# The first two feature tiles computed k by k between the adaLN products, with the input scaling on VectorE and the gate weights summed later

## The chip, the cores and the metric

The kernel runs on one core of a Trainium2 chip. The metric is the device time of one execution in microseconds (us); before the change the median of three runs is 2062.04. The engines are TensorE (PE; PEld is its weight load), VectorE (DVE), ScalarE (ACT), GpSimd (POOL), and SyncE (SP), which issues all DMAs here.

## The reference

One block of a diffusion model over 1024 latent tokens and 256 context tokens of width 1024, in two layers. This case lies in the start of the first (mLSTM) layer:

```python
shift, scale, gate = ada(c, w_ada[i], b_ada[i])            # silu(c) @ w + b, split in three
h_lat = modulate(rmsnorm(x, pre_g), shift, scale)          # h * (1 + scale) + shift
h_ctx = modulate(rmsnorm(ctx, pre_g), c_shift, c_scale)
...
xm, z, og = split(h @ w_in, 3)                             # each 2048 wide
xc = silu(short_conv(xm, conv_w, conv_b))
q, k, v = headwise(xc, w_q), headwise(xc, w_k) * DH**-0.5, headwise(xm, w_v)   # 4x4 blocks
pre = concat(q, k, v) @ w_g + b_g                          # gates of the mLSTM
```

Behind that come the mLSTM scans in two directions, the output projection, and a pooling mixer as second layer. All is fp32; a product is done as three matmuls of split operands (high part by high, high by low, low by high).

## The kernel before

**Layout.** Tokens lie along the free dimension: `x_sb[k]` is the k-th of eight tiles of 128 features by 1024 tokens, `c_sb` holds the context. A *feature tile* n (0 to 15) is 128 of the 2048 columns of `xm`; `features(n, side)` (from L349) computes it in three chunks (512, 512 and 256 tokens), each a sum over the eight k in one PSUM bank, three matmuls per k (`mm3`). It then copies the sums out, convolves them (L372 to L375), splits results into high and low parts and stores them.

**Start.** SP loads x, ctx and sixteen adaLN weight tiles, then the weights of feature tiles 0 and 1 (`first_w`). TensorE's order is written by hand for this stage; `PE_START` (L35) lists it:

```python
PE_START = "0 1 t0 L t1 2 SL t2 C 3 4 t3 5 t4 SC 6 t5 7 t6 t7"
```

A digit n is `ada_product(n)`: two rows of shift and scale for feature block n. `tn` is `ada_turn`: the rows, copied to SBUF by ScalarE, are transposed into columns `mod0[:, n]` and `gs0[:, n]`. `L`, `C` are the token sums of squares, `SL`, `SC` spread the reciprocal norms over the partitions. After that list, x is scaled by its norm: tiles 0 to 4 by VectorE from PSUM (L280), tiles 5 to 7 and the context by GpSimd (L276, L282). Then GpSimd sums the gate weights (L295 to L302): three loads of 512 KB, each multiplied by the 4x4 blocks and added up, giving `gx_all` and `gm_all`. `modulate` (L304) makes each k of the layer's input: ScalarE computes the high part from `src * sc + sh` (L307), VectorE the same in fp32 (L308, a TENSOR_SCALAR) and the low part (L312); the fp32 value is stored to `h_d`.

**Tiles.** Tile 0 is summed with k outside and two chunks inside, so that it can follow `modulate`; from tile 1 on one chunk after the other. While tile n runs, `side` inserts the value products of earlier tiles, one step after each k of tile 2 and after every second k of other tiles. This is `token_part` (L388): its right-hand side `vv` is 128 columns of value weights and 16 gate columns copied from `gm_all` (L397). `gacc` are three PSUM banks (tag `pc`) for the other gate sums. `block_sums` (L503) later reads `h_d` back and forms sums of the blocks of the input for a Strassen product.

TensorE's order is fixed by the program text; on the other engines and on SP a scheduler sets one order per engine when the program is built. An engine executes its instructions in that order, waiting on semaphores. Buffers of a tag rotate: `T5` has five (the adaLN weights 0 to 4, later the gate weights and the convolution's inputs and outputs), `wr`, `wh`, `wl` (loaded weights, their high and low parts) two each. PSUM has eight banks: `pa` 3, `pb` 2, `pc` 3.

Of the kernel before, what the change touches and what calls it, by code (L numbers as in the profile page):

```python
# [17 lines left out]
P = 128  # L18
# [34 lines left out]
def hybrid_block(ctx: ExitStack, tc: tile.TileContext, xT, ctxT, vecs, w_ada0, w_ada, w_blk, w_krow, blk_mask, w_gate, w_in, b_gate, w_out,  # L53
# [32 lines left out]
    def pt_(tag, shape=(P, 512)):  # L86
        return ps.tile(list(shape), F32, tag=tag, bufs=PBUFS[tag], name=nm(tag))

    def const(shape, name, dt=F32):
        return sb.tile(list(shape), dt, name=name)  # L90
# [98 lines left out]
        return row  # L189

    def ada_turn(n, row):
        q = pt_("pc", [P, 2, 2])
        for part in range(2):
            PE.transpose(q[:, part], row[:, part], ident[:2, :2])
        for part in range(2):
            S.activation(mod0[:, n, part], q[:, part], AF.Identity, bias=vc("b_ada0", 8 * part + n))
        S.activation(gs0[:, n], mod0[:, n, 1], AF.Identity, scale=vc("a_pre", n), bias=vc("a_pre", n))
# [88 lines left out]
    gsum = tl("T5", [P, 3, KE, 16])  # L286

    def add4(dst, src):
        G.tensor_tensor(dst, src[:, :, 0], src[:, :, 1], op=ALU.add)
        for o in (2, 3):  # L290
            G.tensor_tensor(dst, dst, src[:, :, o], op=ALU.add)

    for i in range(3):
        g4 = tl("T5", [P, KE, 4, 16])
        nc.sync.dma_start(g4, w_gate[i])  # L295
        G.tensor_tensor(g4, g4, wb[:, i, :, :, None].to_broadcast([P, KE, 4, 16]), op=ALU.mult)
        add4(gsum[:, i], g4)
# [17 lines left out]
    h = {}
    for k in range(KD):
        if k < 4:
            if k % 2 == 0:
                quad = [[tl("S4", [P, 2, 512], F32R) for _ in range(2)] for _ in range(2)]
            for hf in range(2):  # L320
                h[k, hf] = tuple(t[:, k % 2] for t in quad[hf])
            modulate(x_sb[k], [(*h[k, hf], slice(512 * hf, 512 * hf + 512)) for hf in range(2)], k, 0, h_d[k])
        else:
            pair = [tl("S4", [P, T], F32R) for _ in range(2)]
            for hf in range(2):
                h[k, hf] = tuple(t[:, 512 * hf:512 * hf + 512] for t in pair)
            modulate(x_sb[k], [(*pair, slice(0, T))], k, 0, h_d[k])
    hch = [tl("S4", [P, 4, TC], F32R) for _ in range(2)]
    hcl = [tl("S4", [P, 4, TC], F32R) for _ in range(2)]
    for k in range(KD):  # L330
        modulate(c_sb[k // 4][:, k % 4], [(hch[k // 4][:, k % 4], hcl[k // 4][:, k % 4], slice(0, TC))], k, 1)
# [8 lines left out]
    def hx(k, ci, lo):  # L340
        if ci < 2:
            return h[k, ci][lo]
        return (hcl if lo else hch)[k // 4][:, k % 4]


    gacc = [pt_("pc") for _ in range(3)]

    def features(n, side):
        wh, wl = first_w[n] if n < 2 else load_w(w_in[n])  # L349
# [6 lines left out]
        if n == 0:  # L356
            ps_ = [pt_("pa") for _ in range(3)]
            for k, ci in [(k, ci) for k in range(KD) for ci in range(2)] + [(k, 2) for k in range(KD)]:
                mm3(ps_[ci][:, :CHUNKS[ci][1]], wh[:, k], wl[:, k], hx(k, ci, 0), hx(k, ci, 1), k == 0, k == KD - 1)
# [142 lines left out]

    def block_sums():  # L503

        for k in range(4):
# [6 lines left out]
            V.tensor_tensor(b11, b22, b11, op=ALU.add)  # L512
            V.tensor_tensor(b21, b21, b11, op=ALU.subtract)
# [758 lines left out]
```

## Time and profile before

| | |
|---|---|
| median of 3 runs (lowest to highest) | 2062.04 us (2061.18 to 2064.16) |
| the profiled execution | 2061.71 us |
| its span | 2059.9 us |
| busy: PE, PEld | 1993.8, 1680.1 us |
| busy: DVE, ACT, POOL | 1244.8, 760.5, 325.9 us |
| mean granted clock of TensorE | 0.986 of full speed |

Times in the profile count from the start of the span. A row of the timeline gives start, duration, engine, source line (L137 is the matmul helper, so matmuls are told apart by their tiles), operation, output and inputs, how many are merged, and in brackets the idle time before with what ended it. Instructions of one engine may overlap a little, so that rows of merged matmuls add up to slightly more than the time that passed.

### The profile page before, as it was taken

Reading aid. Unit: us, or ns where it says so; the run is one execution under the profiler, and the core shown is the slowest. Engines: PE = TensorE matmul, PEld = TensorE weight load, DVE = VectorE, ACT = ScalarE, POOL = GpSimd, SP = SyncE. Lnnn points to the kernel's source line nnn. Section 1 sums busy time; section 2 is a strip of 40 time slices with the busy share of each in tenths; the row PEclk is TensorE's granted clock in tenths of the full one; section 3 lists DMA queues with packets and bytes.
Section 4 is the critical chain, followed back from the end, with each engine's and each line's share of the span. In section 5 each row is a group of like instructions: output and inputs, shape, how many; then the busy total and the mean of one; then the engine's idle time right before and its main releaser. Section 6 shows DMA issues by size and latency. Waiting matters only on the chain.

```text
span 2059.9 us, 26957 instructions
## 1 busy us (share of the span) xinstructions
PE 1993.8 (97%) x10210; PEld 1680.1 (82%) x10210; DVE 1244.8 (60%) x2115; ACT 760.5 (37%) x1225; POOL 325.9 (16%) x399
## 2 busy tenths in 40 slices
PE   7899999999999899999999999999999999999997
PEld 5678788888888688888888878887888888888897
DVE  4866566677777577667676662444747293844444
ACT  5444454433333432333323322433423131223443
POOL 4400000042232000000000001343000000001265
PEclk9999999999999999999999999999999999999999
DMA  8476776864444854648355334534331312133573
GB/s 322 159 255 222 261 241 214 303 196 138 148 129 133 269 181 141 227 132 273 98 166 207 108 97 144 197 114 163 103 104 50 102 51 92 46 126 130 181 242 124
DMA packets 201986, 339.48 MB, mean 165 GB/s; under 512 B 12508, under 2 KB 116444, under 8 KB 201856
## 3 DMA queue, kind: packets, MB, share of 16 engines
q1 hardware_dynamic: 201856, 337.76, 48.8%
q8 instruction: 80, 1.31, 0.3%
q14 instruction: 50, 0.41, 0.1%
HBM read 234.77 MB, written 102.94 MB: 164 GB/s over the span
## 4 chain that ended last, share of the span: by engine, by line
PE 87%; DVE 3%; DMA 3%; POOL 1%; ACT 1%; issue 1%; SPq 0%; DVEq 0%; ACTq 0%; POOLq 0%
PE pa L137 45%; PE pc L137 33%; PE pb L137 7%; PE pb L781 1%; DMA wr<-in_w_ada_dram 1%; POOL hn L969 1%; PE pc L812 1%; DVE S L901 1%; DVE wl L145 1%; DMA wr<-in_w_in_dram 1%; DMA T<-in_bw_out_dram 0%; DMA S<-xl_d 0%; POOL S L989 0%; DVE wl L658 0%; DMA S<-h_d 0%
## 5 line engine op out<-in xcount | busy, mean ns | idle before, releaser
L137 PE MATMUL pa<-S,wh 128*128 128x512 f32 (+1 forms) x2496 | 725.9, 375 | 13.8 <-DVE S L312 7.1
L137 PEld LDWEIGHTS pa<-S,wh 128*128 128x128 f32 x2496 | 447.4, 191 | 88.6 <-DVE S L312 10.8
L137 PE MATMUL pa<-S,wl 128*128 128x512 f32 (+1 forms) x1248 | 462.5, 371 | 3.3 <-DVE wl L145 3.3
L137 PE MATMUL pc<-S,wh 128*128 128x512 f32 (+1 forms) x1616 | 451.4, 365 | 4.4 <-ACT wh L143 3.5
L137 PEld LDWEIGHTS pc<-S,wh 128*128 128x128 f32 x1616 | 292.7, 189 | 54.3 <-ACT wh L143 3.7
L145 DVE TENSOR_TENSOR wl<-wr,wh 128x1024 fp32r<-128x1024 f32 (+1 forms) x124 | 147.5, 1189 | 273.0 <-ACT wh L143 272.1
L137 PE MATMUL pc<-S,wl 128*128 128x512 f32 (+1 forms) x808 | 293.8, 365 | 1.0 <-DVE wl L145 1.0
L137 PEld LDWEIGHTS pa<-S,wl 128*128 128x128 f32 x1248 | 237.6, 190 | 44.0 <-DVE wl L145 3.7
L137 PE MATMUL pa<-S,S 128*128 128x512 f32 (+1 forms) x1152 | 250.9, 363 | 10.1 <-DMA S<-xh_d 5.8
L143 ACT ACTIVATE wh<-wr 128x1024 fp32r<-128x1024 f32 (+1 forms) x124 | 124.6, 1005 | 368.6 <-PE pa L137 148.3
L137 PE MATMUL pc<-S,pt 128*128 128x512 f32 x960 | 227.4, 391 | 1.5 <-DVE S L721 1.1
L137 PEld LDWEIGHTS pa<-S,S 128*128 128x128 f32 x1152 | 191.8, 190 | 40.2 <-DMA S<-xh_d 6.2
L137 PEld LDWEIGHTS pc<-S,pt 128*128 128x128 f32 x960 | 178.2, 188 | 38.5 <-DVE S L721 1.7
L137 PEld LDWEIGHTS pc<-S,wl 128*128 128x128 f32 x808 | 152.9, 189 | 25.7 <-DVE wl L145 1.8
L783 ACT ACTIVATE pt<-pb 128x512 fp32r<-128x512 f32 (+1 forms) x96 | 47.7, 523 | 213.8 <-PE pb L781 208.0
L969 POOL TENSOR_TENSOR hn<-hn,pt 128x512 f32<-128x512 f32 (+1 forms) x48 | 77.5, 1617 | 309.0 <-ACT pt L968 307.9
L740 DVE SCALAR_TENSOR_TENSOR T<-pa,T 128x256 f32<-128x256 f32 (+3 forms) x184 | 78.2, 454 | 33.5 <-PE pa L137 29.3
L137 PE MATMUL pb<-S,wh 128*128 128x512 f32 x256 | 78.8, 389 | 0.0
L570 ACT ACTIVATE wh<-T 128x512 fp32r<-128x512 f32 x70 | 41.2, 627 | 96.4 <-PE pc L137 78.3
L794 DVE BATCH_NORM_STATS2 st<-pc 128x6 f32<-128x512 f32 x32 | 22.4, 699 | 86.4 <-PE pc L137 86.4
L145 DVE TENSOR_TENSOR wl<-T,wh 128x1024 fp32r<-128x1024 f32 x32 | 45.5, 1421 | 47.3 <-ACT wh L143 47.2
L137 PEld LDWEIGHTS pb<-vv,S 128*128 128x128 f32 x384 | 61.6, 190 | 11.8 <-ACT S L369 1.9
(319 smaller groups left out, 2371.5 us busy)
## 6 DMA issues: line engine op xcount, KB each, us to landing
wr<-in_bw_in_dram SPq DMA_DIRECT2D x40, 512.0 KB, 3.5
wr<-in_w_in_dram SPq DMA_DIRECT2D x34, 512.0 KB, 4.9
wr<-in_w_ada_dram SPq DMA_DIRECT2D x32, 512.0 KB, 4.0
wr<-in_w_out_dram SPq DMA_DIRECT2D x32, 512.0 KB, 3.5
T<-in_bw_out_dram SPq DMA_DIRECT2D x32, 512.0 KB, 4.3
S<-y_d SPq DMA_DIRECT2D x28, 512.0 KB, 7.0
vh_d<-T SPq DMA_DIRECT2D x16, 640.0 KB, 4.0
vl_d<-T SPq DMA_DIRECT2D x16, 640.0 KB, 6.3
```

Of the source, the lines that this page charges most:

```text
L137: PE.matmul(out, lhsT, rhs, start=start, stop=stop)
L143: S.activation(h, r, AF.Copy)
L145: V.tensor_tensor(l, r, f(h), op=ALU.subtract)
L570: S.activation(hi, a, AF.Copy)
L740: V.scalar_tensor_tensor(W[:, lo + sh:hi + sh], p[:, lo - o:hi - o], 1.0, W[:, lo + sh:hi + sh], op0=ALU.mult, op1=ALU.mult, accum_out=dp[ ...
L781: PE.transpose(p[:, j], st["M"][:, s * P:(s + 1) * P], ident)
L783: S.activation(th[:, :n], p[:, :n], AF.Copy)
L794: V.bn_stats(b6, pv)
L812: PE.transpose(p[:, c], hn[:, c * P:(c + 1) * P], ident)
L901: V.tensor_tensor(b, yraw[kp, hf], f(a), op=ALU.subtract)
L969: G.tensor_tensor(acc, acc, sq, op=ALU.add)
```

## The change

- `PE_START` gets steps `F0` to `F7`, one for each k, between and behind the last adaLN products, and each turn comes directly behind its product. `F`k is `early(k)`: it modulates k (latent and context) and adds its part to tiles 0 *and* 1, so six PSUM banks (`pa` and `pc`) are in use at once; `ada_turn` moves from `pc` to `pb`.
- The scaling passes L276, L280 and L282 go. `modulate` multiplies by scale and norm in one SCALAR_TENSOR_TENSOR on VectorE; ScalarE adds the shift for the high part; a second SCALAR_TENSOR_TENSOR gives the low part. `h_d` now holds the value without its shift, which `block_sums` adds.
- The gate weights become a function, called after tile 1; `gacc` is allocated there too.

```diff
-KP = 5
-PE_START = "0 1 t0 L t1 2 SL t2 C 3 4 t3 5 t4 SC 6 t5 7 t6 t7"
+PE_START = "0 1 t0 L t1 2 SL t2 C 3 t3 SC 4 t4 F0 5 t5 F1 6 t6 F2 7 t7 F3 F4 F5 F6 F7"
...
     def ada_turn(n, row):
-        q = pt_("pc", [P, 2, 2])
+        q = pt_("pb", [P, 2, 2])
...
+    def modulate(src, r, parts, k, j, dst=None):
+        sc, sh = gs0[:, k, j:j + 1], mod0[:, k, 0, j:j + 1]
+        V.scalar_tensor_tensor(src, src, sc, r, op0=ALU.mult, op1=ALU.mult)
+        if dst is not None:
+            nc.sync.dma_start(dst, src)
+        for hi, _, c in parts:
+            S.activation(hi, src[:, c], AF.Identity, bias=sh)
+        for hi, lo, c in parts:
+            V.scalar_tensor_tensor(lo, src[:, c], sh, f(hi), op0=ALU.add, op1=ALU.subtract)
...
+    def early(k):
...
+        modulate(x_sb[k], rs_xs, parts, k, 0, h_d[k])
+        modulate(c_sb[k // 4][:, k % 4], rs_cs, [(hch[k // 4][:, k % 4], hcl[k // 4][:, k % 4], slice(0, TC))], k, 1)
+        for n in range(2):
+            if k == 0:
+                ps_[n] = [pt_("pc" if n else "pa") for _ in range(3)]
+            for ci in range(3):
+                mm3(ps_[n][ci][:, :CHUNKS[ci][1]], first_w[n][0][:, k], first_w[n][1][:, k], hx(k, ci, 0), hx(k, ci, 1),
+                    k == 0, k == KD - 1)
...
+        elif step[0] == "F":
+            early(int(step[1]))
...
-    for k in range(KP, KD):
-        G.tensor_tensor(x_sb[k], x_sb[k], rs_xs, op=ALU.mult)
-    for k in range(KP):
-        for ci in range(2):
-            o = ci * 512
-            V.tensor_tensor(x_sb[k][:, o:o + 512], x_sb[k][:, o:o + 512], rs_ps[ci], op=ALU.mult)
-    for k in range(2):
-        G.tensor_tensor(c_sb[k], c_sb[k], rs_cs[:, None, :].to_broadcast([P, 4, TC]), op=ALU.mult)
+
+    def gate_weights():
+        gsum = tl("T5", [P, 3, KE, 16])
...
-    def modulate(src, parts, k, j, dst=None):
-        sc, sh = gs0[:, k, j:j + 1], mod0[:, k, 0, j:j + 1]
-        for hi, _, c in parts:
-            S.activation(hi, src[:, c], AF.Identity, bias=sh, scale=sc)
-        V.tensor_scalar(src, src, sc, sh, op0=ALU.mult, op1=ALU.add)
...
-        for hi, lo, c in parts:
-            V.tensor_tensor(lo, src[:, c], f(hi), op=ALU.subtract)
...
-            V.tensor_tensor(b22, b22, b12, op=ALU.subtract)
+            V.scalar_tensor_tensor(b22, b22, dsh[:, k], b12, op0=ALU.add, op1=ALU.subtract)
...
             out = features(n, side)
             for _ in side:
                 pass
+            if n == 1:
+                gacc.extend(pt_("pc") for _ in range(3))
+                gate_weights()
```

The order of the instructions changes at three places that the prediction uses.

SP, behind the start's loads, before. `S_1_100`, `S_2_102`, ... are the x tiles that go to `h_d`, `T_78_460`, `T_79_466`, `T_80_472` the gate weights, `wr_788` and `wr_1043` the weights of tiles 2 and 3:

```order
L247 DMA bg<-in_b_gate_dram 128x16
L295 DMA T_78_460<-in_w_gate_dram 128x1024
L310 DMA h_d<-S_1_100 128x1024
L310 DMA h_d<-S_2_102 128x1024
L310 DMA h_d<-S_4_106 128x1024
L141 DMA wr_788<-in_w_in_dram 128x1024
L295 DMA T_79_466<-in_w_gate_dram 128x1024
L295 DMA T_80_472<-in_w_gate_dram 128x1024
L141 DMA wr_1043<-in_w_in_dram 128x1024
```

and with the change, where `wr_1214` and `wr_1402` are the weights of tiles 4 and 5, `T_123_749`, `T_124_755`, `T_125_761` the gate weights, `T_107_695` and `T_115_728` the convolved tiles 0 and 1:

```order
L266 DMA h_d<-S_11_120 128x1024
L140 DMA wr_1214<-in_w_in_dram 128x1024
L140 DMA wr_1402<-in_w_in_dram 128x1024
L330 DMA T_123_749<-in_w_gate_dram 128x1024
L377 DMA xc_d<-T_107_695 128x1024
L385 DMA xh_d<-S_109_702 128x1024
L386 DMA xh_d<-pt_701 128x256
L330 DMA T_124_755<-in_w_gate_dram 128x1024
L385 DMA xl_d<-S_110_703 128x1024
L386 DMA xl_d<-pt_701 128x256
L377 DMA xc_d<-T_115_728 128x1024
L330 DMA T_125_761<-in_w_gate_dram 128x1024
```

The gate loads stood ahead of the weights of tile 3; they now stand behind those of tiles 4 and 5 and between the stores of tiles 0 and 1. `wr_1402` takes the buffer that tile 3's weights leave, `T_124_755` that of tile 1's convolution input.

VectorE, at the copies from `gm_all` (`hn_458` before, `hn_677` now) into `vv` of tiles 0 and 1, before:

```order
L370 TENSOR_TENSOR S_107_578<-pa_580,S_106_577 128x512
L397 CAST vv_807<-hn_458 128x2x16
L397 CAST vv_906<-hn_458 128x2x16
L145 TENSOR_TENSOR wl_792<-wr_788,wh_790 128x1024
L370 TENSOR_TENSOR pt_576<-pa_581,pt_576 128x256
```

and with the change:

```order
L144 TENSOR_TENSOR wl_1034<-wr_1030,wh_1032 128x1024
L373 SCALAR_TENSOR_TENSOR T_107_695<-T_103_679,vec,T_107_695 128x1281
L374 SCALAR_TENSOR_TENSOR T_107_695<-T_103_679,vec,T_107_695 128x1281
L373 SCALAR_TENSOR_TENSOR T_115_728<-T_111_712,vec,T_115_728 128x1281
L374 SCALAR_TENSOR_TENSOR T_115_728<-T_111_712,vec,T_115_728 128x1281
L383 TENSOR_TENSOR S_110_703<-T_107_695,S_109_702 128x1024
L383 TENSOR_TENSOR pt_701<-T_107_695,pt_701 128x256
L370 TENSOR_TENSOR pt_716<-pc_398,pt_716 128x256
L370 TENSOR_TENSOR S_114_718<-pc_396,S_113_717 128x512
L370 TENSOR_TENSOR S_114_718<-pc_397,S_113_717 128x512
L383 TENSOR_TENSOR S_118_736<-T_115_728,S_117_735 128x1024
L397 CAST vv_792<-hn_677 128x2x16
```

The copies stood among the copies of tile 0; they now stand behind all the work of tiles 0 and 1.

TensorE, at the start of tile 2 (`pa_786`, weights `wh_775` and `wl_777`), with the change:

```order
L136 MATMUL pc_398<-S_45_205,wl_192 128x256
L136 MATMUL pa_786<-S_70_371,wh_775 128x512
L136 MATMUL pa_786<-S_71_372,wh_775 128x512
L136 MATMUL pa_786<-S_70_371,wl_777 128x512
L136 MATMUL pa_786<-S_70_371,wh_775 128x512
L136 MATMUL pa_786<-S_71_372,wh_775 128x512
L136 MATMUL pa_786<-S_70_371,wl_777 128x512
L136 MATMUL pb_798<-vv_792,S_105_684 128x144 x2
L136 MATMUL pb_798<-vv_792,S_106_685 128x144
```

The first row ends step F7. As before, the first value products of tile 0 (`pb_798` from `vv_792`) follow the second k of tile 2; what stands ahead of tile 2 is now both tiles interleaved.

## Rows read from the trace of the kernel before

**Rows 1.** The page's first part: span, and busy time of TensorE.
```profile
span 2059.9 us, 26957 instructions
...
PE 1993.8 (97%) x10210; PEld 1680.1 (82%) x10210; DVE 1244.8 (60%) x2115; ACT 760.5 (37%) x1225; POOL 325.9 (16%) x399
```

**Rows 2.** Timeline of TensorE: start, duration, line, operation, tiles, count, idle before.
```profile
36.07 7.15 PE L137 MATMUL pb<-S,csil 128*2 128x128 f32 x64
43.15 0.28 PE L194 MATMUL pc<-ident,pt 2*128 2x2 f32 x2
43.36 3.66 PE L137 MATMUL pb<-S,csil 128*2 128x128 f32 x32
...
47.16 0.71 PE L137 MATMUL pa<-ident,rstc 128*128 128x128 f32 x4
...
68.89 0.80 PE L137 MATMUL pa<-S,wh 128*128 128x512 f32 x1 [4.43 <-DVE S L312]
...
83.31 0.73 PE L137 MATMUL pa<-S,wh 128*128 128x512 f32 x2
...
97.20 0.63 PE L137 MATMUL pa<-S,wh 128*128 128x512 f32 x2
...
98.58 0.45 PE L137 MATMUL pb<-vv,S 128*128 128x144 f32 x3
```

**Rows 3.** Windows: each engine's busy time, then granted clock, DMA share, GB/s.
```profile
67.00:70.00 3.00, 1.11 (x3) 0.93 (x4) 3.00 (x3) 0.00 (x0) 3.00 (x3) 0.50 0.19 74
...
76.00:79.00 3.00, 2.64 (x13) 1.92 (x11) 3.00 (x7) 2.10 (x4) 2.85 (x5) 0.83 0.00 0
```

**Rows 4.** Timeline of VectorE.
```profile
41.15 3.22 DVE L308 TENSOR_SCALAR S<-S,gs,mod 128x1024 f32<-128x1024 f32 x2
...
58.48 0.80 DVE L308 TENSOR_SCALAR S<-S,gs,mod 128x1024 f32<-128x1024 f32 x1
...
86.15 1.56 DVE L373 SCALAR_TENSOR_TENSOR T<-T,vec,T 128x1281 f32<-128x1281 f32 x1 [0.34 <-ACT T L372]
```

**Rows 5.** Timeline of ScalarE.
```profile
39.76 0.37 ACT L188 ACTIVATE pt<-pb 2x256 f32<-2x256 f32 x1
...
83.17 1.06 ACT L143 ACTIVATE wh<-wr 128x1024 fp32r<-128x1024 f32 x1 [4.58 <-PE pa L137]
```

**Rows 6.** Timeline of SyncE's queue: second and third load of gate weights.
```profile
56.54 0.86 SPq L295 DMA_DIRECT2D T<-in_w_gate_dram  x2
```

**Rows 7.** Timeline of GpSimd: the gate product that waited for the second load.
```profile
61.07 3.61 POOL L296 TENSOR_TENSOR T<-T,cst 128x1024 f32<-128x1024 f32 x1 [6.27 <-DMA T<-in_w_gate_dram]
```

**Rows 8.** GpSimd's groups, 0 to 100 us: shapes, count, busy us and mean ns, idle before.
```profile
L296 POOL TENSOR_TENSOR T<-T,cst 128x1024 f32<-128x1024 f32 x3 | 8.0, 2654 | 6.3 <-DMA T<-in_w_gate_dram 6.3
L291 POOL TENSOR_TENSOR T<-T,T 128x256 f32<-128x256 f32 x6 | 7.9, 1333 | 0.0
...
L289 POOL TENSOR_TENSOR T<-T 128x256 f32<-128x256 f32 x3 | 3.5, 1179 | 0.1
...
L302 POOL TENSOR_TENSOR hn<-T,hn 128x256 fp32r<-128x256 f32 x2 | 1.6, 832 | 0.0
...
L301 POOL CAST hn<-T 128x256 fp32r<-128x256 f32 x2 | 0.9, 464 | 0.1
L298 POOL TENSOR_SCALAR T<-T 128x256 f32<-128x256 f32 x1 | 0.9, 859 | 0.1
L299 POOL TENSOR_TENSOR T<-T 128x256 f32<-128x256 f32 x1 | 0.9, 851 | 0.1
L238 POOL TENSOR_TENSOR S<-S 128x256 f32<-128x256 f32 x1 | 0.7, 726 | 0.1
```

**Rows 9.** GpSimd's gate sums by line: ns min/median/max, first and last start, shapes.
```profile
L296 POOL TENSOR_TENSOR T<-T,cst x3: 1975/2375/3612, 44.6 to 65.8; 128x1024 f32<-128x1024 f32 x3
...
L289 POOL TENSOR_TENSOR T<-T x3: 777/1057/1702, 47.1 to 69.4; 128x256 f32<-128x256 f32 x3
...
L291 POOL TENSOR_TENSOR T<-T,T x6: 1059/1178/1712, 53.7 to 74.1; 128x256 f32<-128x256 f32 x6
```

More of the change, by code (lines that the diff above doesn't have):

```diff
@@ L252, in hybrid_block, with hx @@
     const([P, 32], "pad1")
+    h = {}
+    hch = [tl("S4", [P, 4, TC], F32R) for _ in range(2)]
+    hcl = [tl("S4", [P, 4, TC], F32R) for _ in range(2)]
+    def hx(k, ci, lo):
+        if ci < 2:
+            return h[k, ci][lo]
+        return (hcl if lo else hch)[k // 4][:, k % 4]
+    def modulate(src, r, parts, k, j, dst=None):
[7 more added lines that the diff above has]
+            V.scalar_tensor_tensor(lo, src[:, c], sh, f(hi), op0=ALU.add, op1=ALU.subtract)
+    ps_, quad = {}, []
+    def early(k):
+        if k < 4:
+            if k % 2 == 0:
+                quad[:] = [[tl("S4", [P, 2, 512], F32R) for _ in range(2)] for _ in range(2)]
+            for hf in range(2):
+                h[k, hf] = tuple(t[:, k % 2] for t in quad[hf])
+            parts = [(*h[k, hf], slice(512 * hf, 512 * hf + 512)) for hf in range(2)]
+        else:
+            pair = [tl("S4", [P, T], F32R) for _ in range(2)]
+            for hf in range(2):
+                h[k, hf] = tuple(t[:, 512 * hf:512 * hf + 512] for t in pair)
+            parts = [(*pair, slice(0, T))]
+        modulate(x_sb[k], rs_xs, parts, k, 0, h_d[k])
[6 more added lines that the diff above has]
+                    k == 0, k == KD - 1)
     rows = {}
@@ L259, in hybrid_block @@
         elif step == "SL":
-            rs_ps = [pt_("pa") for _ in range(2)]
+            rs_xs = tl("S4", [P, T])
             for ci in range(2):
-                spread(rs_ps[ci], rl, 4 * ci, 4)
+                p = pt_("pa")
+                spread(p, rl, 4 * ci, 4)
+                S.activation(rs_xs[:, ci * 512:ci * 512 + 512], p, AF.Copy)
         elif step == "SC":
-            rs_c = pt_("pa", [P, TC])
-            spread(rs_c, rc_, 0, 2)
+            p = pt_("pa", [P, TC])
+            spread(p, rc_, 0, 2)
@@ L277, in hybrid_block, with add4 @@
-    for k in range(KP):
-        for ci in range(2):
-            o = ci * 512
-            V.tensor_tensor(x_sb[k][:, o:o + 512], x_sb[k][:, o:o + 512], rs_ps[ci], op=ALU.mult)
-    for k in range(2):
-        G.tensor_tensor(c_sb[k], c_sb[k], rs_cs[:, None, :].to_broadcast([P, 4, TC]), op=ALU.mult)
+    def gate_weights():
+        gsum = tl("T5", [P, 3, KE, 16])
+        def add4(dst, src):
+            G.tensor_tensor(dst, src[:, :, 0], src[:, :, 1], op=ALU.add)
+            for o in (2, 3):
+                G.tensor_tensor(dst, dst, src[:, :, o], op=ALU.add)
+        for i in range(3):
+            g4 = tl("T5", [P, KE, 4, 16])
+            nc.sync.dma_start(g4, w_gate[i])
+            G.tensor_tensor(g4, g4, wb[:, i, :, :, None].to_broadcast([P, KE, 4, 16]), op=ALU.mult)
+            add4(gsum[:, i], g4)
+        G.tensor_scalar(gsum[:, 1], gsum[:, 1], QSCALE, None, op0=ALU.mult)
+        G.tensor_tensor(gsum[:, 0], gsum[:, 0], gsum[:, 1], op=ALU.add)
+        for dst, i in ((gx_all, 0), (gm_all, 2)):
+            G.tensor_copy(dst[:, :, 0:16], gsum[:, i])
+            G.tensor_tensor(dst[:, :, 16:32], gsum[:, i], f(dst[:, :, 0:16]), op=ALU.subtract)
@@ L284, in hybrid_block @@
     gx_all = tl("hn", [P, KE, 32], F32R)
     gm_all = tl("hn", [P, KE, 32], F32R)
[L286 to L297, printed above, removed]
@@ L315, in hybrid_block @@
[L315 to L327, printed above, removed]
@@ L328, in hybrid_block @@
[L328 to L331, printed above, removed]
     def bilinear():
@@ L338, in bilinear @@
         V.tensor_scalar(amat, amat, QSCALE, None, op0=ALU.mult)
[L340 to L346, printed above, removed]
+    gacc = []
     def features(n, side):
@@ L355, in features @@
         xml = [tl("S4", [P, T], F32R), cp[:, 1]]
[L356 to L359, printed above, removed]
         for ci, (o, w) in enumerate(CHUNKS):
-            p = pt_("pa") if n else ps_[ci]
-            for k in range(KD if n else 0):
+            p = pt_("pa") if n > 1 else ps_[n][ci]
+            for k in range(KD if n > 1 else 0):
                 mm3(p[:, :w], wh[:, k], wl[:, k], hx(k, ci, 0), hx(k, ci, 1), k == 0, k == KD - 1)
@@ L503, in block_sums @@
     def block_sums():
+        dsh = const1([P, 4, 1], "dsh")
+        V.tensor_tensor(dsh, mod0[:, 4:8, 0, 0:1], mod0[:, 0:4, 0, 0:1], op=ALU.subtract)
         for k in range(4):
```

15 lines of the change are left out of this document (3 added, 12 removed).

## The prediction

> **What bounds the kernel now.** I read the page's busy shares first [rows 1]: TensorE is busy for 97% of the span, so a change pays only where TensorE stands still or runs at a lower clock. Then TensorE's instructions over the first 100 us [rows 2], since everything the change moves lies there. The reader is to see three stretches: eight adaLN products (the fourth starts at 36.07, and one alone takes 3.66), then feature tile 0, broken by waits for VectorE (the longest is 4.43 us, before 68.89), then tile 1 without a wait from 83.31 to 97.20. One more row decides the forecast: at 98.58, two k-steps into tile 2, TensorE starts the value products of tile 0. Their right-hand side `vv` holds gate weights, and here they had long been ready. [...] VectorE's and GpSimd's rows tell why tile 0 waited: while GpSimd scales and sums, a TENSOR_SCALAR of 1024 elements takes 1.61 us on VectorE, against 0.80 at 58.48 when GpSimd waited for a load [rows 4, 7].
>
> From the three positions in the order shown with the change I take one thing: the state of the work at the first `vv` product is the same before and after (tiles 0 and 1 finished, two k-steps of tile 2 done), and behind it the engines' orders agree. So the change is worth the shift of that moment, which was 98.58, plus the clock lost around it.
>
> **Term 1: tiles 0 and 1 end earlier.** The fourth product's start, 36.07, is untouched. Then each product is followed by its own turn, which is no longer covered by the next product: copy to SBUF 0.37 [rows 5], transposes 0.28 [rows 2], some 0.15 of hand-overs (my estimate): 0.8. That gives 36.07 + 3.66 + 0.8 = 40.5, context spread 0.71 to 41.2, product 3.66 to 44.9, turn to 45.7. Step F0 could start there. It needs VectorE's last weight subtraction for tile 1, however. VectorE starts at about 36.1 and has before it: four 1024-element SCALAR_TENSOR_TENSOR (the only one shown took 1.56 for 1281, so 1.25), four of 512 (0.62), six of 256 (about 0.35 each by the same rate), two weight subtractions (1.25): 5.0 + 2.5 + 2.1 + 2.5 = 12.1, so 48.2, with small ones 48.6. The rest of F0 behind it is about 1.3: F0 ends at 50.0. One F step is two tiles' share of one k: tile 1 took 97.20 - 83.31 = 13.9 for eight, so 3.47 for both. Left are three products with turns (13.4) and seven steps (24.3): end E = 50.0 + 13.4 + 24.3 = 87.7, against 97.20. The scaling that GpSimd did and the TENSOR_SCALARs become work of VectorE. I cost that at nothing after F0: VectorE needs about 28 us for all of it and TensorE takes over 50 from 36 to E. If each instruction took double, that cover is gone (a rival below).
>
> **Term 2: tile 2 starts with its weights unconverted.** Before, that conversion hid under tile 1. Now its buffers come free only at the last step: ScalarE 1.06 [rows 5], VectorE 1.25, so about 2.3 before the first weight-remainder product; the two k-steps end near E + 3.2 = 90.9. With nothing else in the way the first `vv` product would come 7.7 us earlier than before.
>
> **Term 3: the gate weights are late.** Their three loads stand on SP behind the weight loads of tiles 4 and 5. SP issues in order, and the second of those waits until VectorE has split tile 3's weights: two ScalarE copies and one subtraction behind E, 1.06 + 1.06 + 1.25 = 3.4. SP spends 0.43 for one issue and a gate load took 61.07 - 56.54 = 4.5 to land [rows 6, 7]: E + 8.3 = 96.0 for the first. GpSimd then works alone. The shortest duration of each kind [rows 8, 9] gives three products of 1.98, three adds of 0.78, six of 1.06, and 0.86 + 0.85 + 0.93 + 1.66 for the rest: 18.9. The first group of 4.9 ends at 100.9. The second load reuses the buffer of tile 1's convolution input: it is issued behind four 1281-element VectorE instructions, E + 3.4 + 6.2 + 0.4 = 97.7, and lands at 102.2, 1.3 after GpSimd could use it. Left are 14.0: 116.2. VectorE's copy into `vv` and the hand-overs, 0.4 by estimate: 116.6. Behind that copy VectorE's queue holds nothing that could let TensorE go on, and TensorE's own order allows nothing else. It stands still for some 25.7 us. I take the shortest durations because VectorE, whose work lengthened the others, is itself waiting for most of this stretch. The upper end is the busy total of the same rows, 23.7.
>
> For a 256-element operation the row of GpSimd with VectorE idle shows 0.73, and the shortest gate add 1.06 [rows 8, 9]. [...]
>
> **Term 4: the clock.** After a stop of 4.43 the products from 68.89 ran at half clock until about 76.7, a loss of 3.9 [rows 2, 3]; part of that stretch was lengthened by more waits. One window of 3 us at 0.50 would lose 1.5. I take 3.0, nearer the first, since this stop is longer.
>
> **The rest.** Twelve three-operand instructions replace two-operand ones in the block sums of tiles 2 and later, 512 elements each, under feature products: nothing; if each took 0.6 more and none were hidden, 7 us. Zero cost too for the PSUM banks of the gate sums, which tile 1's copies free during the stop.
>
> **Sum.** 116.6 - 98.58 = 18.0, and 3.0 for the clock: +21.0. The profiled execution took 2061.71 (span 2059.9), 0.3 under the median of 2062.04, so 2082.7.
>
> **Rivals.**
> *GpSimd held back by VectorE.* For it: 3.61 for one gate product beside a busy VectorE, 1.98 for another [rows 9]. Against it: VectorE is done with tiles 0 and 1 some 15 us after E. With the mean durations [rows 8] the first group takes 6.5, to 102.5, and 17.2 are left: 120.1 with the copy, +21.5 + 3.0, 2086. [...]
> [...]
> *VectorE is the bound.* The rate of SCALAR_TENSOR_TENSOR stands on one row. At double, 28 us become 56, from 36.1 to 92; the last step ends at 95.6 and all shifts by 8: 2091. GpSimd's absence speaks against it.
> *Not slower: the stop doesn't come.* If the gate sums were ready by 90.9, the kernel would gain 7.7, 2054. The deciding point is a resumption before 95.6 (98.58 less the clock's 3.0). For it: the first load's own buffer is free since the third product. Against it: SP's order, and the second and third loads take buffers that tiles 0 and 1 use themselves. A stop cut to a few us would give no difference.
>
> **How the numbers follow.** About 0.2%, 4 us, is what a measurement of this kernel tells from no change. Chances: forecast 0.56, GpSimd held back 0.17, GpSimd quicker 0.15, VectorE the bound 0.05, not slower 0.07 (faster 0.04, same 0.03). Slower thus 0.93. The range takes in the first three: downward from 2081, less 1.5 for the clock's lower end and less 4.5 should F0 not be held (0.8), the turns be covered after all (2.4) and the second load land when GpSimd asks for it (1.3), 2075; upward from 2086 with 0.9 for the clock's upper end and 3 for an E that half clock between the steps delays, 2090. About 0.12 are left out with the other two.
>
> **What would show it.** Right: no wait over 2 us in steps F1 to F7, E near 88; VectorE's first CAST into `vv` waiting for GpSimd and TensorE idle for over 20 us at its first `vv` product; half clock behind it; from there on the same stretches as before. Wrong: the first gate load issued before step F7; the `vv` products starting before 105; waits for SCALAR_TENSOR_TENSOR in F4 to F7; or a difference that arises after 150 us.

## The result, and the profile after

The changed kernel takes 2080.93 us (median of 4 runs, 2078.87 to 2081.75), the kernel before 2062.61 beside it: a ratio of 1.0087, 95% interval 1.007 to 1.0105. The prediction said 2082.7, from 2075 to 2090, and slower. The profiled execution of the changed kernel took 2081.2 us, 19.5 more than that of the kernel before; its span is 2079.4 against 2059.9.

The page of the changed kernel, first part and one group of part 5 (the matmuls of the value products: busy, mean ns, idle time ahead of them and what ended most of it):

```profile
span 2079.4 us, 26941 instructions
...
PE 1993.0 (96%) x10210; PEld 1681.9 (81%) x10210; DVE 1232.9 (59%) x2106; ACT 759.7 (37%) x1225; POOL 309.1 (15%) x394
...
L136 PE MATMUL pb<-vv,S 128*128 128x144 f32 x384 | 59.6, 265 | 27.2 <-DVE vv L397 25.6
```

TensorE is busy for as long as before [rows 1]; what came is idle time. Of the 27.2 us ahead of all 384 value products, 25.6 ended with VectorE's copy into `vv`, and TensorE's timeline shows them to be one stop:

```profile
35.82 3.65 PE L136 MATMUL pb<-S,csil 128*2 128x128 f32 x32
...
46.12 0.28 PE L193 MATMUL pb<-ident,pt 2*128 2x2 f32 x2 [1.62 <-ACT pt L187]
50.01 3.65 PE L136 MATMUL pb<-S,csil 128*2 128x128 f32 x32
54.13 0.28 PE L193 MATMUL pb<-ident,pt 2*128 2x2 f32 x2 [0.46 <-ACT pt L187]
...
88.33 0.73 PE L136 MATMUL pa<-S,wh 128*128 128x512 f32 x2 [0.31 <-ACT wh L142]
89.59 0.50 PE L136 MATMUL pa<-S,wl 128*128 128x512 f32 x1 [0.53 <-DVE wl L144]
...
116.38 0.89 PE L136 MATMUL pb<-vv,S 128*128 128x144 f32 x3 [25.59 <-DVE vv L397]
118.44 0.75 PE L136 MATMUL pb<-vv,S 128*128 128x144 f32 x3
120.33 0.46 PE L136 MATMUL pb<-vv,S 128*128 128x144 f32 x3
```

These answer to [rows 2]. F0 ends at 50.0, and no F step after it waits for VectorE. Tiles 0 and 1 end at 88.0 (tile 2's first matmul, 88.33, less its wait of 0.31), 9.2 us earlier than before. TensorE is ready for the first `vv` product at 90.8 (116.38 less 25.59), 7.8 earlier than before, and gets it 17.8 later. The chain behind that stop, in the order SP, GpSimd, VectorE:

```profile
89.56 1.82 SPq L140 DMA_DIRECT2D wr<-in_w_in_dram  x2
91.44 0.42 SPq L330 DMA_DIRECT2D T<-in_w_gate_dram  x1
...
97.63 0.91 SPq L330 DMA_DIRECT2D T<-in_w_gate_dram  x1
```

```profile
96.88 2.32 POOL L331 TENSOR_TENSOR T<-T,cst 128x1024 f32<-128x1024 f32 x1 [54.34 <-ACT S L382]
...
102.72 2.88 POOL L331 TENSOR_TENSOR T<-T,cst 128x1024 f32<-128x1024 f32 x1
...
110.97 0.72 POOL L334 TENSOR_TENSOR T<-T 128x256 f32<-128x256 f32 x1
...
115.30 0.72 POOL L337 TENSOR_TENSOR hn<-T,hn 128x256 fp32r<-128x256 f32 x1
```

```profile
97.33 2.95 DVE L383 TENSOR_TENSOR S<-T,S 128x1024 fp32r<-128x1024 f32 x1
...
102.60 1.21 DVE L383 TENSOR_TENSOR S<-T,S 128x1024 fp32r<-128x1024 f32 x1
...
116.05 0.27 DVE L397 CAST vv<-hn 128x32 fp32r<-128x32 f32 x2 [10.17 <-POOL hn L337]
```

The first gate load goes out at 91.44, behind the weight loads of tiles 4 and 5. GpSimd starts 5.4 us later and is done at 116.0; VectorE waits 10.17 us for it, makes its copy, and TensorE goes on. (The bracket at 96.88 names a ScalarE copy that ended near that time. No operand of that product comes from it; the profile gives a gate load here 4.3 to 5.3 us from issue to landing, so the load is the likelier cause.) The windows give the clock, in the column after POOL's:

```profile
88.00:93.00 5.00, 1.95 (x7) 0.97 (x6) 4.60 (x6) 4.91 (x9) 0.00 (x0) 1.00 0.38 111
93.00:97.00 4.00, 0.00 (x0) 0.00 (x0) 3.90 (x3) 3.55 (x5) 0.12 (x1) 0.50 0.84 311
...
116.00:120.00 4.00, 3.62 (x12) 3.17 (x13) 0.27 (x2) 0.00 (x0) 0.02 (x1) 0.50 0.01 4
120.00:123.00 3.00, 3.00 (x19) 2.63 (x18) 0.67 (x2) 0.49 (x1) 0.00 (x0) 0.95 0.00 0
```

The granted clock is 0.50 from 93 us on, through the rest of the stop, and back near full speed before 123 (0.95 from 120 to 123, 1.00 from 123 to 126). Two steps of one `vv` product and one k-step took 3.95 us (116.38 to 120.33); at full clock two take 2.06 (120.33, 121.36, 122.39 are starts of the next ones). So the clock cost 1.9 us, and 17.8 + 1.9 = 19.7 is, to 0.2, the 19.5 of the spans.

### The profile page after: what moved, and what is told of

The parts are those of the page before. It is cut to its first block, busy times and chain, and to the rows that moved or that the text cites. A ratio compares the mean times of both kernels' runs of the same rounds, so it can differ in the third digit from the quotient of the medians.

```text
span 2079.4 us, 26941 instructions
## 1 busy us (share of the span) xinstructions
PE 1993.0 (96%) x10210; PEld 1681.9 (81%) x10210; DVE 1232.9 (59%) x2106; ACT 759.7 (37%) x1225; POOL 309.1 (15%) x394
## 4 chain that ended last, share of the span: by engine, by line
PE 84%; DMA 5%; DVE 4%; POOL 3%; issue 2%; ACT 1%; SPq 0%; DVEq 0%; POOLq 0%; ACTq 0%
PE pa L136 43%; PE pc L136 32%; PE pb L136 7%; PE pb L787 1%; DMA wr<-in_w_ada_dram 1%; POOL S L995 1%; POOL hn L975 1%; PE pc L818 1%; DMA S<-in_w_ada_dram 1%; DMA S<-in_ctxT_dram 0%; DVE wl L664 0%; DVE S L907 0%; DMA T<-in_bw_out_dram 0%; DMA S<-xl_d 0%; DVE T L746 0%
## 5 line engine op out<-in xcount | busy, mean ns | idle before, releaser
L136 PE MATMUL pa<-S,wh 128*128 128x512 f32 (+1 forms) x2448 | 709.8, 375 | 5.3 <-DVE pt L370 5.0
L136 PEld LDWEIGHTS pa<-S,wh 128*128 128x128 f32 x2448 | 437.9, 190 | 75.0 <-DVE pt L370 5.6
L136 PE MATMUL pc<-S,wh 128*128 128x512 f32 (+1 forms) x1664 | 464.5, 365 | 3.9 <-ACT wh L142 3.1
L136 PE MATMUL pa<-S,wl 128*128 128x512 f32 (+1 forms) x1224 | 453.5, 371 | 3.9 <-DVE wl L144 3.9
L136 PEld LDWEIGHTS pc<-S,wh 128*128 128x128 f32 x1664 | 301.2, 189 | 55.1 <-ACT wh L142 3.3
L136 PE MATMUL pc<-S,wl 128*128 128x512 f32 (+1 forms) x832 | 302.3, 365 | 1.0 <-DVE wl L144 1.0
L136 PEld LDWEIGHTS pa<-S,wl 128*128 128x128 f32 x1224 | 232.4, 190 | 44.8 <-DVE wl L144 4.7
L136 PEld LDWEIGHTS pc<-S,wl 128*128 128x128 f32 x832 | 157.3, 189 | 26.6 <-DVE wl L144 1.8
L136 PEld LDWEIGHTS pb<-vv,S 128*128 128x128 f32 x384 | 62.8, 194 | 37.6 <-issue 26.0
L136 PE MATMUL pb<-vv,S 128*128 128x144 f32 x384 | 59.6, 265 | 27.2 <-DVE vv L397 25.6
L410 DVE TENSOR_TENSOR T<-pb,T 128x384 fp32r<-128x384 f32 x64 | 31.3, 490 | 72.8 <-ACT T L409 72.7
```

The lines of the kernel that those rows point to most:

```text
L136: PE.matmul(out, lhsT, rhs, start=start, stop=stop)
L410: V.tensor_tensor(vl[:, s0:s1], q[:, :, :P], f(vh[:, s0:s1]), op=ALU.subtract)
```

## The experiments

The fourth adaLN product starts between 34.5 and 37.8 us in the executions profiled, ahead of all that the change moves. So positions are counted from that start in this table: "ready" is the end of tiles 0 and 1 (tile 2's first matmul less its wait), "vv" the start of the first `vv` product. Ratios are to the kernel before.

| kernel | fourth product | ready | vv | median us | ratio (95%) |
|---|---|---|---|---|---|
| before | 36.1 | 61.1 | 62.5 | 2062.6 | 1 |
| changed | 35.8 | 52.2 | 80.6 | 2080.9 | 1.0087 (1.007 to 1.0105) |
| no gate sums | 35.9 | 53.0 | 55.6 | 2057.7 | 0.9976 (0.9967 to 0.9986) |
| gates early, GpSimd | 37.8 | 60.3 | 62.9 | 2063.1 | 1.0005 (0.9992 to 1.0017) |
| gates early, VectorE | 34.5 | 52.1 | 54.7 | 2054.6 | 0.9962 (0.9949 to 0.9975) |
| before, gates late | 35.5 | 50.2 | 72.5 | 2074.4 | 1.0061 (1.0044 to 1.0078) |
| before, scaling on VectorE | 34.7 | 61.4 | 62.8 | 2059.5 | 0.9989 (0.998 to 0.9998) |
| gate loads first | 37.8 | 52.2 | 79.1 | 2079.1 | 1.0084 (1.0069 to 1.01) |
| filler matmuls | 34.8 | 52.1 | 80.8 | 2077.8 | 1.0079 (1.0063 to 1.0096) |
| VectorE, vv 4 steps later | 34.5 | 52.1 | 58.1 | 2048.7 | 0.9939 (0.9918 to 0.9959) |

**1. No gate sums at all.** What is the interleave worth when nothing stops it?

```diff
+    for dst in (gx_all, gm_all):
+        G.tensor_copy(dst, zero1[:, :, None].to_broadcast([P, KE, 32]))
...
-                gate_weights()
```

> The changed kernel without the gate sums: the gate weights are neither loaded nor summed, zeros stand in their place (so the gates are their biases alone). Theory (interleave worth 7.7 us, the stop and its clock loss are the gate sums alone): first vv product near 91 us, no stretch at half clock longer than 3 us behind it, 2052 to 2056 us. Rival (part of the loss lies in the interleave itself, in the half-clock steps or the unconverted weights of tile 2): 2060 us or more without any gate sums.

Measured: 2057.7. The first `vv` product came where it was expected, but the time is above the 2052 to 2056 expected. TensorE's timeline shows a second stop, before the third group of `vv` products, and a granted clock of 0.55 behind it (from 100 to 104 us; steps of 2.06 and 1.92 instead of 1.03):

```profile
91.47 0.45 PE L136 MATMUL pb<-vv,S 128*128 128x144 f32 x3
...
100.47 0.89 PE L136 MATMUL pb<-vv,S 128*128 128x144 f32 x3 [2.65 <-DVE pre L411]
...
102.53 0.75 PE L136 MATMUL pb<-vv,S 128*128 128x144 f32 x3
```

`pb` has two banks in this program (`PBUFS`). The third group needs the first one's, which is free once VectorE has subtracted (L410) and added to `pre` (L411). On VectorE's queue those stand behind the convolutions of both tiles, which now arrive together:

```profile
93.59 1.55 DVE L374 SCALAR_TENSOR_TENSOR T<-T,vec,T 128x1281 f32<-128x1281 f32 x1
95.06 1.55 DVE L373 SCALAR_TENSOR_TENSOR T<-T,vec,T 128x1281 f32<-128x1281 f32 x1
96.72 1.55 DVE L374 SCALAR_TENSOR_TENSOR T<-T,vec,T 128x1281 f32<-128x1281 f32 x1
98.19 1.22 DVE L383 TENSOR_TENSOR S<-T,S 128x1024 fp32r<-128x1024 f32 x1
...
100.12 0.20 DVE L411 TENSOR_TENSOR pre<-pre,pb 128x48 f32<-128x48 f32 x1
```

So the late gate sums are the whole loss. Without any gate sums, the rest of the change is 4.9 us faster than the kernel before, not 7.7. How much of that is the interleave, and how much comes from GpSimd no longer summing beside tile 0, as it does in the kernel before, this run doesn't tell; experiment 4 bears on it. In the changed kernel VectorE did this work during the long stop, so that the second one doesn't show there.

**2. Gate sums early, on GpSimd as before.**

```diff
+    gate_weights()
     side, parts, sums = iter(()), [], block_sums()
...
-                gate_weights()
```

> The changed kernel with the gate weights summed where they were before the change: the function is called ahead of the feature tiles, so that its three loads stand on SP's queue ahead of the weight loads of tiles 2 to 5. Theory (the whole loss is the late gate sums): the sums are ready before E + 3 us, TensorE starts the first vv product near 91 us instead of 116.4, stands still there for under 3 us, and the kernel takes 2054 to 2060 us (2054 by 98.58 - 90.9 = 7.7 under the time before; up to 2060 if GpSimd beside VectorE lengthens the F steps as it did in the kernel before). Rival (GpSimd beside VectorE costs the interleave its whole gain: VectorE's instructions double while GpSimd sums): F steps wait for VectorE by several us each, the first vv product starts at 98 or later, and the kernel takes 2062 us or more. Second rival (the stop was not the gate sums but something else behind tile 1): TensorE still idles over 20 us there and the time stays at 2081.

Measured: 2063.1, no difference from before. (The profiled execution took 2068.4, the longest of ten; its fourth product is late by 1.7.) The stop at the first `vv` product is gone (ready 60.3, `vv` 62.9), but so is the gain ahead of it: tiles 0 and 1 end 8.1 us later than in the changed kernel. The first rival was right. VectorE's timeline, GpSimd's, and a window of TensorE behind its longest wait:

```profile
41.37 5.07 DVE L270 SCALAR_TENSOR_TENSOR S<-S,mod,S 128x512 fp32r<-128x512 f32 x4
```

```profile
42.64 2.11 POOL L331 TENSOR_TENSOR T<-T,cst 128x1024 f32<-128x1024 f32 x1 [0.23 <-DMA T<-in_w_gate_dram]
...
45.96 2.71 POOL L326 TENSOR_TENSOR T<-T,T 128x256 f32<-128x256 f32 x2
```

```profile
51.00:53.00 2.00, 1.84 (x6) 1.54 (x7) 2.00 (x5) 2.00 (x5) 0.00 (x0) 0.56 0.34 43
```

Four SCALAR_TENSOR_TENSOR of 512 elements take 1.27 us each beside GpSimd's gate sums (0.68 each in the next experiment, without them), and the GpSimd adds 1.36 each instead of 0.72. TensorE waited for ScalarE's copies behind that work, 4.70 us before its turn at 51.16 and 2.44 before that at 70.67 (1.62 and 0.46 in the changed kernel). These waits make 5.1 of the 8.1 us; the other 3.0 are the F steps behind them, which ran in part at a lower clock (0.56 from 51 to 53 us). Two explanations were left: the two engines hinder each other, or VectorE simply has no room.

**3. Gate sums early, by VectorE itself.** The same operations behind F1, all `G.` turned into `V.`:

```diff
+        elif step == "G":
+            gate_weights()
-"... F0 5 t5 F1 6 t6 F2 ..."
+"... F0 5 t5 F1 G 6 t6 F2 ..."
-            G.tensor_tensor(dst, src[:, :, 0], src[:, :, 1], op=ALU.add)
+            V.tensor_tensor(dst, src[:, :, 0], src[:, :, 1], op=ALU.add)
```

> The changed kernel with the gate sums done early and by VectorE: the same operations, issued behind F1, all on VectorE in the slack of the F steps, none on GpSimd. Theory (the early gate sums of the first experiment ate the interleave's gain because GpSimd and VectorE slow each other, not because there is too much work): VectorE's 1024-element SCALAR_TENSOR_TENSOR stays at 1.2 to 1.3 us each, its own gate work is 8 to 12 us in all, tiles 0 and 1 end at 88 to 91 us, the first vv product starts at 91 to 94.5 us, the stop of about 2.6 us before the third group of vv products is there as without any gate sums, and the kernel takes 2057 to 2061 us. Rival (VectorE's work is the bound of the F steps as soon as the gate sums lie there, whoever does them): F steps wait for VectorE by over 4 us in sum, tiles 0 and 1 end at 95 or later, 2063 us or more.

Measured: 2054.6, under the 2057 to 2061 expected; tiles 0 and 1 end at 86.6 and the first `vv` product starts at 89.3, both a little ahead of what was expected. VectorE's timeline:

```profile
38.11 2.73 DVE L270 SCALAR_TENSOR_TENSOR S<-S,mod,S 128x512 fp32r<-128x512 f32 x4
...
57.51 1.21 DVE L307 TENSOR_TENSOR T<-T,cst 128x1024 f32<-128x1024 f32 x1
```

With more work on VectorE and none on GpSimd, tiles 0 and 1 end at 52.1, as in the changed kernel (52.2), and TensorE has no wait over 0.53 us between F0 and the first `vv` product. A gate product takes 1.21 us here and 1.93 on GpSimd; the gate sums come to some 9 us of VectorE (three products, nine adds at 0.37 to 0.41, 2.0 for the rest). So VectorE had the room, and it was the two engines side by side that cost 8 us in experiment 2. The stop before the third group is 2.72 us. That this kernel came out under the one without gate sums is not settled: the two intervals overlap.

Not all of the 8 us lie in the stretch that was changed. In the profiled executions this kernel is 3.4 us ahead of the kernel before at the end of a stop that both have (137.44 against 140.81), and 8.2 at the end of the span. Most of the rest arises at the next such stop, in the kernel before and here:

```profile
242.82 1.22 PE L137 MATMUL pa<-S,wh 128*128 128x512 f32 x2 [4.38 <-DVE pt L370]
```

```profile
235.92 0.74 PE L136 MATMUL pa<-S,wh 128*128 128x512 f32 x2 [2.43 <-DVE pt L372]
```

There the kernel before stands 4.38 us and goes on at a granted clock of 0.50 (242 to 246 us), with 1.22 for the first two matmuls; this one stands 2.43 and takes 0.74 for them. Why that stop came out shorter, no run here shows.

**4. The kernel before, gate sums late.** One part of the change alone:

```diff
+    def gate_weights():
+        gsum = tl("T5", [P, 3, KE, 16])
...
+            if n == 1:
+                gate_weights()
```

> The kernel before with one part of the change alone: the gate weights in a function called after tile 1; scaling and the adaLN products stay as before. Theory (late gate sums cost by themselves): GpSimd no longer slows VectorE in tile 0, so that tile 1 ends at 84 to 93 us instead of 97.2; but the first gate load is issued near the end of tile 1 and TensorE stands still before its first vv product for 20 us or more; that product starts at 112 to 121 instead of 98.58, and the kernel takes 2075 to 2086 us. Rival (the stop needs the interleave, which takes the PSUM and weight buffers of both tiles at once): the loads go out during tile 1 and the stop is under 8 us, 2062 us or less.

Measured: 2074.4, so this part alone costs 12 us. The theory holds in kind; its numbers were too high, 108.0 for the first `vv` product against 112 at least, and 2075 at least for the time. Rows of SP, GpSimd and TensorE:

```profile
82.84 1.07 SPq L296 DMA_DIRECT2D T<-in_w_gate_dram  x1
```

```profile
87.39 2.46 POOL L297 TENSOR_TENSOR T<-T,cst 128x1024 f32<-128x1024 f32 x1 [31.28 <-ACT pt L370]
```

```profile
108.03 0.89 PE L137 MATMUL pb<-vv,S 128*128 128x144 f32 x3 [20.82 <-DVE vv L398]
```

From GpSimd's start to the first `vv` product are 20.6 us, in the changed kernel 19.5: the price of the sums is nearly the same, and what differs is when the first load goes out, here before tile 1's end (85.7), there 3.4 after it. Counted from the fourth product the load goes out 8.3 us earlier here (47.3 against 55.6) and the first `vv` product starts 8.1 earlier. With GpSimd not summing beside VectorE, tiles 0 and 1 end at 50.2 without any interleave, even before the changed kernel's 52.2. So what held tile 0 in the kernel before was GpSimd's gate sums, not the order of the k. It follows that no run here shows the interleave itself to bring anything: with the gate sums late in both, the kernel with the old order (and its scaling on GpSimd) ends tiles 0 and 1 2.0 us earlier than the one with the new order; with them early on GpSimd in both (experiment 2), the new order ends 0.8 us earlier and takes the same time. The obvious rival to experiments 3 and 8, the kernel before with its gate sums early on VectorE, was not run.

**5. The kernel before, all scaling on VectorE.** The other part alone:

```diff
-    for k in range(KP, KD):
-        G.tensor_tensor(x_sb[k], x_sb[k], rs_xs, op=ALU.mult)
-    for k in range(KP):
+    for k in range(KD):
...
-        G.tensor_tensor(c_sb[k], c_sb[k], rs_cs[:, None, :].to_broadcast([P, 4, TC]), op=ALU.mult)
+        V.tensor_tensor(c_sb[k], c_sb[k], rs_cs[:, None, :].to_broadcast([P, 4, TC]), op=ALU.mult)
```

> The kernel before with the other part alone: all eight x tiles and the context are scaled by VectorE in passes of their own, with no scaling on GpSimd; the gate sums stay where they were. Theory (the scaling alone is worth a few us either way and is not where the 19 us come from): GpSimd begins the gate sums earlier, VectorE has about 4 us more to do before tile 0 can go on, and the first vv product moves by less than 4 us from 98.58; 2058 to 2066 us. Rival (VectorE's larger share is what the change costs): tile 0 waits for VectorE by 8 us or more in addition, 2070 us or more.

Measured: 2059.5, ratio 0.9989 (0.998 to 0.9998); the first `vv` product stays (62.8 against 62.5). That agrees with the theory: from the fourth product, GpSimd's second gate product starts 6.5 us earlier (53.19 less 34.72, against 61.07 less 36.07), VectorE has some 6 us more to do, and the two nearly cancel.

**6. The changed kernel, gate loads first on SP.**

```diff
+            if n == 0:
+                gate_weights()
             if n == 1:
                 gacc.extend(pt_("pc") for _ in range(3))
-                gate_weights()
```

> The changed kernel with one move: the gate weights are summed behind feature tile 0 in the program, not behind tile 1, which puts the first gate load on SP ahead of the weight loads of tiles 4 and 5, and the other two right behind them, with buffers that tile 0 and 1 do not need. Theory (SP's order and the buffers set how late the stop ends, by term 3): the first load goes out near 83 us, GpSimd's first group is done by 95, the second load lands near 96 instead of 102.2, 14 us of sums are left, and the first vv product starts near 110.5 instead of 116.4; 2075 us. Rival (GpSimd's pace, held back by VectorE's work behind tiles 0 and 1, sets it): the sums stretch by the time won, the first vv product stays at 114 to 117 and the time at 2079 to 2081.

Measured: 2079.1, `vv` 1.5 us earlier. The theory's 6 us did not come; the time is the rival's, though GpSimd's pace is only a part of the cause. SP, GpSimd, and TensorE's restart:

```profile
93.38 3.34 SPq L330 DMA_DIRECT2D T<-in_w_gate_dram  x2
```

```profile
79.26 1.94 POOL L331 TENSOR_TENSOR T<-T,cst 128x1024 f32<-128x1024 f32 x1 [36.86 <-DMA T<-in_w_gate_dram]
...
101.01 4.00 POOL L331 TENSOR_TENSOR T<-T,cst 128x1024 f32<-128x1024 f32 x2 [17.14 <-DMA T<-in_w_gate_dram]
```

```profile
116.83 0.89 PE L136 MATMUL pb<-vv,S 128*128 128x144 f32 x3 [24.10 <-DVE vv L397]
...
122.73 0.49 PE L136 MATMUL pb<-vv,S 128*128 128x144 f32 x3
```

The first group was done early, beside the F steps, without delaying them. But the second load still stands behind both weight loads, landed 7.6 us after its issue instead of 4.5, and left GpSimd idle for 17.14 us. The sums behind it then ran beside the convolution of tile 1 and took 15.5 us to the end, where 14.0 were reckoned. The first load's place on SP was not what set the end; the second load's was, and the GpSimd work behind it.

**7. Filler matmuls in the stop.** 105 matmuls ahead of the first `vv` product keep TensorE at work:

```diff
+                if n == 0 and s == 0:
+                    d = pt_("pb")
+                    for _ in range(105):
+                        mm(d, ah, xmh[0][:, 0:512], True, True)
```

> The changed kernel with 105 matmuls of 512 columns put ahead of the first vv product, into a PSUM bank that nobody reads: they fill some 24 us of TensorE's stop and need nothing that is late. Theory (term 4: work behind the stop is slow only because the granted clock fell while TensorE stood still): the first vv product stays near 116.4, the clock is at full speed behind it, the half-clock stretch of 116.4 to about 120 us goes, and the kernel takes 1.5 to 2.5 us less than the changed kernel, 2078.5 to 2079.5. Rival (the clock falls for another reason, the start of the stretch itself): half clock behind the vv product as before, and no less time, 2080.5 or more.

Measured: 2077.8 (ratio 1.0079, 1.0063 to 1.0096), 3 us under the changed kernel where 1.5 to 2.5 were expected; the two intervals overlap, so the size is not settled by the times. The trace is plain. TensorE, then the window behind it:

```profile
89.45 23.96 PE L136 MATMUL pb<-S 128*128 128x512 f32 x105
115.62 0.56 PE L136 MATMUL pb<-vv,S 128*128 128x144 f32 x3 [2.20 <-DVE vv L397]
```

```profile
116.00:118.00 2.00, 2.00 (x14) 1.75 (x14) 0.00 (x0) 0.00 (x0) 0.00 (x0) 1.00 0.00 0
```

The first `vv` product is where it was (80.8 from the fourth product, 80.6 in the changed kernel), the clock is 1.00 in all windows of this stretch (0.50 in the changed kernel from 116 to 120 us), and the following steps are 1.03 apart. Term 4's cause, that the clock fell because TensorE stood still, is shown.

**8. The third group's stop taken away.** On experiment 3, `side` begins after the sixth k-step of tile 2:

```diff
-                if n == 2 or k % 2:
+                if (n == 2 and (ci or k > 4)) or (n != 2 and k % 2):
                     next(side, None)
```

> The kernel with the gate sums on VectorE in the F steps, and one thing more: in tile 2 the value products begin after the sixth k-step instead of the second, so four k-steps (2.8 us) later; what does not fit into tile 2 runs at its end. Theory (the stop of 2.72 us before the third group, and the half clock behind it, are there because its PSUM bank is given back only after VectorE has convolved both tiles): the third group asks for its bank 2.8 us later, the stop shrinks to under 0.5 us, the clock stays full, and with 2.7 us of stop and some 3.5 us of half clock gone the kernel takes 2047 to 2051 us. Rival (the stop only moves: VectorE's work behind tile 1 or the flush at the end of tile 2 stops TensorE for as long): 2053 us or more.

Measured: 2048.7, ratio 0.9939 (0.9918 to 0.9959). TensorE at the third group (the seventh `vv` step), and a window:

```profile
98.80 0.45 PE L136 MATMUL pb<-vv,S 128*128 128x144 f32 x3
```

```profile
100.00:104.00 4.00, 4.00 (x27) 3.19 (x27) 3.88 (x11) 2.63 (x7) 0.00 (x0) 1.00 1.00 392
```

No wait, and a clock of 1.00: the stop is gone, not moved. Stop and lower clock (0.50 from 100 to 104 us in experiment 3) had cost 4.7 us by the ratios (0.9962 - 0.9939) or 5.9 by the medians, for an idle time of 2.72. The two ratio intervals overlap, so the times alone don't settle the size. The traces bear it out: with the fourth product at 34.5 in both, the next stop (before 137.44 in experiment 3, before 132.10 here) begins 5.8 us earlier here. With eight steps instead of four (`n == 2 and ci`):

> As the run before, with the value products beginning after the whole first chunk of tile 2 (eight k-steps, six later than in the changed kernel, 4.1 us). Theory: no stop before the third group; more of the steps is left for the end of tile 2, where nothing lies between them, so that evictions of the value products may be waited for there by some tenths of a us each: 2047 to 2052 us, not below the run with four steps. Rival (the stop only moves): 2053 us or more.

Measured: 2049.5, ratio 0.9946 (0.9929 to 0.9964); one wait of 1.22 us is new, at 112.45. The two can't be told apart. Either beats the kernel before by 0.5 to 0.6%, and the changed one by some 1.5% (1.0087 / 0.9939).

## Why the prediction was right

*Term 1, tiles 0 and 1 end at 87.7.* Measured 88.0. F0 ended at 50.0 as forecast, but not by the path reckoned, so that agreement is partly luck. The prediction let F0 wait for VectorE's last weight subtraction. The trace shows no wait inside F0; what held it was the turn ahead of it, at 46.12, after a wait of 1.62 that was not foreseen. ScalarE's copy for that turn stood behind work that had waited for VectorE's scaling. Rows of ScalarE, VectorE and TensorE:

```profile
43.95 0.91 ACT L268 ACTIVATE S<-S,mod 128x256 fp32r<-128x256 f32 x2 [1.58 <-DVE S L264]
```

```profile
47.16 1.21 DVE L144 TENSOR_TENSOR wl<-wr,wh 128x1024 fp32r<-128x1024 f32 x1
```

```profile
48.65 0.40 PE L136 MATMUL pc<-S,wl 128*128 128x512 f32 x1
```

The subtraction ended at 48.37, 0.3 us before its first reader at 48.65. With the turn on time it would have been what held F0, to an end within some 0.3 us of the same (my estimate from these rows). A turn takes less than the 0.8 (its wait 0.46, transposes and the start of the F step within 0.7). "Nothing after F0" held for the changed kernel, and experiment 2 shows its condition: with GpSimd beside it, VectorE takes 1.27 us instead of 0.68 for a SCALAR_TENSOR_TENSOR of 512 elements, and 8 us come back. That is the case of the rival "VectorE is the bound", which "GpSimd's absence speaks against".

*Term 2, ready for `vv` at 90.9.* Measured 90.8.

*Term 3, first `vv` product at 116.6 after 25.7 idle.* Measured 116.38 after 25.59. Two errors inside it cancel. GpSimd started 0.9 later than 96.0, and the first group, which ran beside VectorE's last subtractions (2.95 us for one that takes 1.21), took 5.7 instead of 4.9. What came behind, with VectorE waiting, went at 0.72 to 0.78 an add, where the sum had 0.78 and 1.06: 13.3 from 102.72, not 14.0, although its first product, still beside VectorE, took 2.88 instead of 1.93. The wait of 1.3 us for the second load did not show: the longer first group covered it. So the rival "GpSimd held back by VectorE" was right for the first group and not for the rest. The range is counted down from 2081, for a GpSimd quicker in all its groups; no run shows that price. The run shows in its place a first group of 5.7 us, 13.3 behind it and, with that, nearly the stop that was forecast.

*Term 4, 3.0 for the clock.* Measured 1.9, inside its bounds of 1.5 to 3.9; this is the term that was mis-sized, and with 0.2 from term 3 it makes 1.3 of the 1.5 us by which the profiled execution (2081.2) stayed under 2082.7. I had taken a longer stop to mean more half clock behind it; the run shows 3.9 us at a granted clock of 0.50 after 25.59 idle. The loss does not go by the length of the stop: after the 24.10 us of experiment 6 three steps took 5.9 us instead of 3.1 (116.83 to 122.73), a loss of 2.8.

*The rest at nothing.* Behind 123 us no new stretch shows: at the next stop that both kernels have, the changed one is 19.7 us behind (160.55 against 140.81), and 19.5 at the end.

*A rival's price was wrong.* "The stop doesn't come" was put at 2054. Experiment 1 made that case and took 2057.7; a stop before the third group is there that the price left out, since the two tiles' work arrives on VectorE at once. Experiment 3's 2054.6 is no confirmation: it has that stop too, and more than half of its lead arises behind the changed stretch. I had named their 1281-element instructions as a delay for a load, but not asked who else waits behind them.

*Why the two engines slow each other.* The rows of experiments 2 and 3 show that they do (1.27 against 0.68 us for VectorE's operation of 512 elements), and so does the changed kernel (2.95 against 1.21 for VectorE's subtraction; 0.72 for a GpSimd add with VectorE waiting, against 1.36 in experiment 2); why, no run here shows.

## What to carry to other kernels

Before moving work "later, off the start", look for its first consumer, and at the queue on which its loads would then stand: here 19 us of side work on an idle engine became a stop of the busy one, with the interleave (25.59 us) and without it (20.82 us). When two tiles are finished together, the engine behind gets two tiles' work in one piece; what it must give back soon (here a PSUM bank) stands behind all of it, and shifting the consumer by four steps took away a stop that had cost some 5 us. When a change has several parts, run them apart: the part that gave it its name, the interleave, is not shown to bring anything here. Work that hinders a neighbour may be cheaper on that neighbour: 19 us of gate sums on GpSimd were 9 us on VectorE, and the F steps ended 8 us earlier than beside GpSimd.

## What the runs showed of the hardware that was not expected

- A short stop cost twice its length: 2.65 and 2.72 us idle before the third group (experiments 1 and 3) were followed by a granted clock of 0.55 and 0.50 (100 to 104 us in both; in experiment 3 the three steps from 98.31 to 104.20 took 5.9 us, at full clock 3.1). 2.20 us in experiment 7 left the clock at 1.00 (116 to 126 us), 2.08 us in the kernel before (before 140.81) did not (0.50 from 142 to 145 us), and 25.59 and 24.10 us cost only 1.9 and 2.8 us behind the stop.
- In the kernel before, removing GpSimd's gate sums from the first tiles brought their end 10.9 us forward (61.1 to 50.2, experiment 4) with no other edit.
